# One level of Strassen in the MLP's up-projection: 19 of 22 tile pairs per layer

## The chip, the core and the metric

One core of a Trainium2 chip runs the whole trunk as one program. The metric is the device time in microseconds. TensorE multiplies matrices, VectorE and ScalarE do the elementwise work, GpSimd is nearly unused, and SyncE issues the transfers.

## The reference, cut to what matters

Two encoder layers over 512 tokens of width 1024 in float32. Each layer has four token mixers, one output projection, and then a gated MLP:

```python
h = rms_norm(x, ffn_norm_g[i])
u = depthwise_conv(h @ w_up, conv_w, conv_b)     # 1024 -> 2 x 2816, width-3 conv over tokens
gate, up = jnp.split(u, 2, axis=-1)
x = x + (silu(gate) * up) @ w_down               # 2816 -> 1024
```

A final RMSNorm closes the trunk.

## The kernel before, in words

Everything lies transposed: channels in the 128 partitions, the 512 tokens in the free dimension. A float32 product is made of three reduced-precision products (`float32r`): each operand is split into a high half (`hi`, a cast) and a low half (`lo`, the difference, always on VectorE), and hi x hi, hi x lo and lo x hi are accumulated in PSUM (`mm3`). The cast (`copy`) may go to ScalarE or VectorE, as the planner likes.

The MLP of a layer (`ffn`) goes through 22 pairs of up tiles: tile 2j is the gate's 128 channels, tile 2j+1 the matching up channels. `up_tile` loads 512 KB of weights (128 x 1024), splits them, does 8 x 3 products of 128x512 on the not yet normalised input, scales the result out of PSUM by the norm factor `r` (`evac_r`), and applies the width-3 convolution (one ScalarE and two VectorE instructions). `pair` applies silu, multiplies, and splits the product for the down projection. After every part of `PARTS = (5, 6, 6, 5)` pairs, `down` multiplies that part with its rows of the down weights, 8 output tiles, and adds each into the residual `x`. The last part of the last layer is done by `finish`, in two halves of 256 tokens, with the final norm. During layer 0's MLP a generator (`side`, `s5_prep`) records the preparation of layer 1's state-space weights after the pairs.

The order of issue is not the recorded order. Class `_Plan` records all instructions and then makes a list schedule: each instruction has a cost from `_cost`, ten forward and backward passes set priorities, and a buffer can be taken only if one is free. Buffers are 49 small slots of SBUF (`NSLOT`, up to 515 words a partition), 19 large ones (`NBIG`, 1024 words and a little more), tiny ones and 8 PSUM banks; weights have caps on how many are alive (`CAPS`). Each engine then runs its part in that order. All instructions are emitted from one line, L527, so groups of the profile are told apart by tiles (`v_s` a small slot, `v_b` a large one, `v_t` a tiny one, `bank` PSUM, `xs__65` the residual, `vec__67` per-channel vectors) and by shape.

Of the kernel before, what the change touches and what calls it, by code (L numbers as in the profile page):

```python
# [17 lines left out]
P = 128  # L18
D = 1024
S = 512  # L20
# [3 lines left out]
NPAIR = DFF // P  # L24
PARTS = (5, 6, 6, 5)
OUTP = ((3,), (0, 1, 2))
CAPS = (3, 5, 5)
ORDER = ("SGCMpsgcym", "SGCMsgcym")
EARLY = (4, 5)
# [25 lines left out]
CSTW = _off  # L55
NSLOT = 49
NBIG = 19
SLOTW = S + 3
# [8 lines left out]
class _Ap:  # L67
# [19 lines left out]
    def window(self, dims, offset):  # L87
        """A view with its own strides."""
        return _Ap(self.base, self.chain + (("window", (dims, offset), {}),), _window(self.proto, dims, offset))
# [31 lines left out]
class _Plan:  # L121
    """Records instructions, then issues them in the order of a list schedule.

    Buffers live in arenas of SBUF and in the banks of PSUM from their first write to their last use;
    Tile derives every wait from the order of issue."""

# [73 lines left out]
    def tiled(self, mms):  # L200
        """Matrix products in column tiles of the array, which run side by side."""
        d = max(_cost("T", *m)[4] for m in mms) + 53.0 * (len(mms) - 1)
        return self.add([("T", "group", mms, {}, d, 0.0, 0.0)])
# [38 lines left out]
    def settle(self):  # L242
        """Classes of the buffers where the instructions run in the order of recording."""
        left, users, home = dict(self.limit), {}, {}
# [62 lines left out]
    def forward(self, prio, ref, home, horizon):  # L307
        """One list schedule. ref is an order that fits the buffers: an instruction may run ahead of it
        only where the rest of ref still fits, so that no schedule gets stuck."""
        import bisect  # L310
# [49 lines left out]
        def fits(op):  # L360
            """The classes for the buffers that op would take, or None."""
            got, need, upto = [], {}, {}
# [185 lines left out]
def _cost(e, fn, a, k):  # L548
    n = _free(a[0])
    dma = 0.0  # L550
    if e == "T":
        if fn == "transpose":
            d = 109.0
        elif a[1].proto.dtype == F32R:
            d = max(n, 256) / 2.4 + 3.0
        else:
            d = 4.0 * max(n, 128) / 2.4 + 4.0
# [33 lines left out]
def trunk_kernel(  # L591
# [31 lines left out]
    fing_ = const.tile([P, KT], F32, name="fing_")  # L623
    vec_ = const.tile([P, L, VECW], F32, name="vec_")
    slots = ctx.enter_context(tc.tile_pool(name="slots", bufs=1))
    banks = [psp.tile([P, S], F32, name=f"bank{i}") for i in range(8)]
# [14 lines left out]
    def ps(shape=(P, S)):  # L641
        return plan.buf("ps", shape, F32)
# [14 lines left out]
    for k in range(KT):  # L657
        lead.append(X.dma_start(x[k], xT[k * P:(k + 1) * P, :]))
    fing = plan.fixed(fing_[:, :])
    X.dma_start(fing, fin_g)  # L660

# [10 lines left out]
    def wget(src, n, cap=True):  # L672
        raw = sb(F32, (P, n), ("raw", CAPS[0]) if cap else None)
        hi = sb(F32R, (P, n), ("whi", CAPS[1]) if cap else None)
        lo = sb(F32R, (P, n), ("wlo", CAPS[2]) if cap else None)
        plan.loaded = X.dma_start(raw, src)
        copy(hi, raw)
        V.tensor_sub(lo, raw, hi.bitcast(F32))
        return hi, lo
# [40 lines left out]
    def colsum(acc, mat=None):  # L720
        """Sums over the partitions, in every partition."""
        p_ = ps(acc.shape)
        T.matmul(p_, ones if mat is None else mat, acc)
        return p_
# [377 lines left out]
    def attend(scores, vt):  # L1102
        """Two heads; their outputs side by side in the partitions."""
        pt = [[b4(F32, (P, 2, S)) for _ in range(2)] for _ in range(2)]
# [35 lines left out]
    def group_norm(l, grp, y):  # L1140
        """y is the group, but twice that for group 0."""
        r = rstd(sumsq(y), 1024 if grp == 0 else 256)
# [14 lines left out]
    def mixing(l):  # L1157
# [224 lines left out]
        for grps in OUTP:  # L1382
# [3 lines left out]
            for m in range(KT):  # L1386
# [3 lines left out]
                V.tensor_add(x[m], x[m], p_)  # L1390

    def ffn(l, side):
        xh, xl, r = prenorm(l, "ffn_g")
        fw, _ = VEC["fc_w"]
        fb, _ = VEC["fc_b"]

        def up_tile(i):
            w = wget(w_up[l, i], KT * P)
            p_ = ps()
            mm3(p_, w, range(KT), xh, xl, P, P)  # L1400
            u = evac_r(p_, r)

            def cw(k):
                return vecs[l][:, fw + 3 * i + k:fw + 3 * i + k + 1]

# [6 lines left out]
        def pair(j):  # L1412
            g_ = up_tile(2 * j)
            u_ = up_tile(2 * j + 1)
            A.activation(g_, g_, AF.Silu)
            V.tensor_mul(g_, g_, u_)
            return split(g_)
# [13 lines left out]
        def finish(k0, n):  # L1431
            """The last part of the last layer and the norm after it, in two halves of the tokens."""
            ph = {k: prods[k0 + k][0] for k in range(n)}
# [25 lines left out]
        for n in PARTS:  # L1459
            for j in range(n):  # L1460
                prods.append(pair(base + j))
                next(side, None)
                if j == 1 and pend is not None:
                    down(*pend)
                    pend = None
# [160 lines left out]
```

## Time and profile before

| | |
|---|---|
| device time, median of 3 runs | 1248.66 us (1248.66 to 1249.28) |
| span of the profiled execution | 1248.9 us |
| TensorE / VectorE / ScalarE busy | 98% / 74% / 49% of the span |
| HBM read, over the span | 118.96 MB, 106 GB/s with writes |

The profiled execution has its span alone as its time; it lies 0.2 us above the median of the runs. Busy time of TensorE is that of pipelined instructions, so what a product costs is read from many of them in a row, not from the duration of one.

### The profile page before, as it was taken

Reading aid. Unit: us, or ns where it says so; the run is one execution under the profiler, and the core shown is the slowest. Engines: PE = TensorE matmul, PEld = TensorE weight load, DVE = VectorE, ACT = ScalarE, POOL = GpSimd, SP = SyncE. Lnnn points to the kernel's source line nnn. Section 1 sums busy time; section 2 is a strip of 40 time slices with the busy share of each in tenths; the row PEclk is TensorE's granted clock in tenths of the full one; section 3 lists DMA queues with packets and bytes.
Section 4 is the critical chain, followed back from the end, with each engine's and each line's share of the span. In section 5 each row is a group of like instructions: output and inputs, shape, how many; then the busy total and the mean of one; then the engine's idle time right before and its main releaser. Section 6 shows DMA issues by size and latency. Waiting matters only on the chain.

```text
span 1248.9 us, 15868 instructions
## 1 busy us (share of the span) xinstructions
PE 1222.4 (98%) x5824; PEld 937.8 (75%) x5824; DVE 926.8 (74%) x1706; ACT 615.2 (49%) x983; POOL 6.9 (1%) x27
## 2 busy tenths in 40 slices
PE   7999899999999999999999999999999999999996
PEld 5875456878888878888888756668888888888886
DVE  8889988868899665665677998887666656557465
ACT  6448689654443352333352666985533333234223
POOL 0000000000000000000000000000000000000000
PEclk9999999999999999999999999999999999999999
DMA  8559461332223332432555156234223332322211
GB/s 303 148 187 268 107 156 36 134 119 89 71 77 101 101 131 92 123 95 73 187 188 179 53 140 148 64 102 133 87 67 99 109 96 89 99 102 76 83 45 68
DMA packets 71662, 144.38 MB, mean 116 GB/s; under 512 B 20256, under 2 KB 28960, under 8 KB 71456
## 3 DMA queue, kind: packets, MB, share of 16 engines
q1 hardware_dynamic: 71584, 143.37, 37.5%
q8 instruction: 46, 0.75, 0.2%
q14 instruction: 32, 0.26, 0.1%
HBM read 118.96 MB, written 13.89 MB: 106 GB/s over the span
## 4 chain that ended last, share of the span: by engine, by line
PE 88%; DVE 5%; ACT 3%; DMA 1%; issue 1%; SPq 1%; ACTq 0%; DVEq 0%
PE bank L527 88%; DVE v_s L527 4%; ACT v_s L527 2%; DVE v_b L527 1%; DMA v_b<-v_b 1%; ACT L527 1%; SPq L527 1%; ACT v_b L527 1%; DVE v_t L527 0%; DMA xs__65<-in_xT_dram 0%; DMA v_s<-y_d 0%; ACTq L1621 0%; DVEq L1621 0%; ACTq L527 0%
## 5 line engine op out<-in xcount | busy, mean ns | idle before, releaser
L527 PE MATMUL bank<-v_s,v_b 128*128 128x512 f32 (+3 forms) x4594 | 1041.0, 396 | 11.6 <-ACT v_b L527 8.6
L527 PEld LDWEIGHTS bank<-v_s,v_b 128*128 128x128 f32 (+2 forms) x4594 | 794.8, 183 | 219.4 <-issue 25.7
L527 DVE TENSOR_TENSOR v_b<-v_b,v_b 128x1024 fp32r<-128x1024 f32 (+4 forms) x208 | 217.2, 1051 | 33.2 <-PE bank L527 18.2
L527 ACT CAST v_b<-v_b 128x1024 fp32r<-128x1024 f32 (+2 forms) x184 | 168.8, 934 | 114.8 <-PE bank L527 85.1
L527 DVE TENSOR_TENSOR v_s<-v_s,v_s 128x512 f32<-128x512 f32 (+6 forms) x294 | 179.9, 627 | 26.1 <-ACT v_s L527 23.2
L527 DVE TENSOR_TENSOR v_s<-bank,v_s 128x512 f32<-128x512 f32 (+1 forms) x119 | 83.0, 701 | 139.6 <-PE bank L527 137.5
L527 ACT ACTIVATE v_s<-v_s,vec__67 128x512 f32<-128x512 f32 x87 | 71.0, 817 | 195.3 <-DVE v_s L527 192.2
L527 DVE SCALAR_TENSOR_TENSOR v_s<-v_s,vec__67,v_s 128x511 f32<-128x511 f32 (+8 forms) x201 | 148.6, 746 | 15.3 <-ACT v_s L527 9.7
L527 ACT ACTIVATE v_s<-v_s 128x512 f32<-128x512 f32 (+2 forms) x124 | 71.1, 587 | 80.3 <-DVE v_s L527 79.4
L527 DVE TENSOR_TENSOR xs__65<-xs__65,bank 128x512 f32<-128x512 f32 x88 | 59.5, 682 | 61.5 <-PE bank L527 61.5
L527 ACT CAST v_s<-v_s 128x512 fp32r<-128x512 f32 (+1 forms) x70 | 40.0, 585 | 72.9 <-DVE v_s L527 71.4
L527 ACT ACT_TABLE_LOAD x52 | 66.7, 1283 | 15.7 <-DVE v_s L527 7.6
L527 PE MATMUL bank<-v_b,v_b 96*128 96x512 f32 (+5 forms) x264 | 74.1, 450 | 0.0
L527 PE MATMUL bank<-c_sb,v_s 128*128 128x128 f32 x368 | 64.8, 278 | 1.3 <-ACT v_s L527 1.2
L527 PEld LDWEIGHTS bank<-c_sb,v_s 128*128 128x128 f32 x368 | 44.6, 140 | 27.5 <-issue 18.5
L527 PE MATMUL bank<-v_b,v_s 128*128 128x64 f32 (+4 forms) x268 | 60.7, 393 | 1.9 <-ACT v_s L527 1.2
L527 PE MATMUL bank<-v_s,v_s 128*64 128x128 f32 (+2 forms) x258 | 57.4, 348 | 1.4 <-ACT v_s L527 1.4
L527 ACT ACTIVATE v_s<-bank,v_t 128x512 f32<-128x512 f32 x68 | 46.5, 697 | 10.6 <-DVE v_t L527 10.5
L527 PEld LDWEIGHTS bank<-v_b,v_s 128*128 128x128 f32 (+1 forms) x268 | 34.0, 173 | 16.0 <-issue 7.7
L527 DVE TENSOR_REDUCE v_t<-bank 128x1 f32<-128x512 f32 x64 | 42.3, 681 | 4.4 <-PE bank L527 3.7
L527 PEld LDWEIGHTS bank<-v_b,v_b 96*128 96x128 f32 (+3 forms) x264 | 33.2, 165 | 16.5 <-issue 8.1
L527 PEld LDWEIGHTS bank<-v_s,v_s 128*128 128x128 f32 (+1 forms) x258 | 32.1, 165 | 14.9 <-issue 5.7
(82 smaller groups left out, 517.9 us busy)
## 6 DMA issues: line engine op xcount, KB each, us to landing
v_b<-in_w_up_dram SPq DMA_DIRECT2D x88, 512.0 KB
v_b<-in_w_in_dram SPq DMA_DIRECT2D x28, 512.0 KB
v_b<-in_w_dn_dram SPq DMA_DIRECT2D x32, 384.0 KB
v_b<-in_w_dn_dram SPq DMA_DIRECT2D x32, 320.0 KB
v_b<-v_b SPq DMA_DIRECT2D x24, 256.0 KB
v_b<-in_w_out_dram SPq DMA_DIRECT2D x16, 384.0 KB
v_s<-x_d SPq DMA_DIRECT2D x22, 257.5 KB
v_s<-wt_d SPq DMA_DIRECT2D x15, 256.0 KB
```

The source lines that it names most:

```text
L527: self.issued(op, getattr(eng[e], fn)(*[res(z) for z in a], **{n: res(z) for n, z in k.items()}))
```

## The change

Of the 22 pairs of a layer the first three (`DIRECT`) stay as they are, with their weights loaded and split in blocks of 128 x 512. For each of the other 19, the pair's weights are a 2 x 2 matrix of blocks (two tiles by two halves of the 1024 inputs) and the input is a 2 x 2 matrix (two halves of the inputs by two halves of the tokens, 256 each). Seven block products replace eight (Winograd's form of Strassen): four sums of weight blocks are made per pair, and the sums of the input blocks (`operands`) once per layer, on the normalised input. Each product is 4 x 3 products of 128x256. The results are put together in PSUM, by ScalarE copies and by VectorE additions. The up tile comes out negative, and its convolution weights are negated once per layer (`nfw`). The down projection runs in 6 parts, (4, 4, 4, 4, 3, 3). There are 51 small and 22 large slots, new caps for the blocks' weights, and the planner's cost of a product is 0.4453 ns per column + 4 ns instead of 1/2.4 + 3. The scratch memory for descriptors is set to 2048.

```diff
-PARTS = (5, 6, 6, 5)
+PARTS = (4, 4, 4, 4, 3, 3)
+DIRECT = 3
+WCAPS = (10, 9, 9)
-NSLOT = 49
-NBIG = 19
+NSLOT = 51
+NBIG = 22
...
-            d = max(n, 256) / 2.4 + 3.0
+            d = 0.4453 * max(n, 256) + 4.0
...
+    def blocks(l, j):
+        w = [[sb(F32, (P, 512), ("sw", WCAPS[0])) for _ in range(2)] for _ in range(2)]
+        for i in range(2):
+            for h in range(2):
+                X.dma_start(w[i][h], w_up[l, 2 * j + i, :, 512 * h:512 * h + 512])
+        return w
...
+        V.tensor_scalar(nfw, vecs[l][:, fw:fw + 6 * NPAIR], -1.0, None, ALU.mult)
+        H = S // 2
+        CW = ("sh", WCAPS[1]), ("sl", WCAPS[2])
+        def operands():
+            q = {}
+            for kh, nh in ((0, 0), (0, 1), (1, 0), (1, 1)):
+                t_ = q[kh, nh] = b4(shape=(P, 4, H))
+                for k in range(4):
+                    V.scalar_tensor_tensor(t_[:, k], x[4 * kh + k][:, H * nh:H * nh + H], vcol(l, "ffn_g", 4 * kh + k),
+                                           r[:, H * nh:H * nh + H], ALU.mult, ALU.mult)
+            b11, b12, b21, b22 = q[0, 0], q[0, 1], q[1, 0], q[1, 1]
+            n1, n2, t4 = (b4(shape=(P, 4, H)) for _ in range(3))
+            V.tensor_sub(n1, b11, b12)
+            f11 = halves(b11)
+            V.scalar_tensor_tensor(n2, n1, -1.0, b22, ALU.mult, ALU.subtract)
+            fn1 = halves(n1)
+            V.scalar_tensor_tensor(t4, n2, -1.0, b21, ALU.mult, ALU.subtract)
+            f21, fn2 = halves(b21), halves(n2)
+            V.tensor_sub(b12, b22, b12)
+            return dict(b11=f11, b21=f21, n1=fn1, n2=fn2, b22=halves(b22), t3=halves(b12), t4=halves(t4))
+        def product(out, w, f, start):
+            for k in range(4):
+                sl = slice(k * P, k * P + P)
+                T.matmul(out, w[0][:, sl], f[0][:, k], start=start and k == 0, stop=False, skip_group_check=True)
+                T.matmul(out, w[0][:, sl], f[1][:, k], start=False, stop=False, skip_group_check=True)
+                T.matmul(out, w[1][:, sl], f[0][:, k], start=False, stop=(k == 3), skip_group_check=True)
+        def quarters(j):
+            a, c = blocks(l, j)
+            s1, s2_, s3, s4 = (sb(F32, (P, 512), ("sw", WCAPS[0])) for _ in range(4))
+            V.tensor_add(s1, c[0], c[1])
+            V.tensor_add(s2_, s1, a[0])
+            V.tensor_add(s3, a[0], c[0])
+            V.tensor_add(s4, s2_, a[1])
+            w11, w12, w1, w2, w4, w3, w22 = (halves(z, *CW) for z in (a[0], a[1], s1, s2_, s4, s3, c[1]))
+            g_, u_ = s2(), s2()
+            xb, yb, zb = (ps((P, H)) for _ in range(3))
+            product(xb, w11, ops["b11"], True)
+            A.activation(g_[:, 0:H], xb, AF.Copy)
+            product(zb, w12, ops["b21"], True)
+            V.tensor_add(g_[:, 0:H], g_[:, 0:H], zb)
+            product(yb, w1, ops["n1"], True)
+            A.activation(u_[:, H:S], yb, AF.Copy)
+            product(xb, w2, ops["n2"], False)
+            A.activation(g_[:, H:S], xb, AF.Copy)
+            product(yb, w4, ops["b22"], False)
+            V.tensor_add(g_[:, H:S], g_[:, H:S], yb)
+            product(xb, w3, ops["t3"], False)
+            V.tensor_add(u_[:, H:S], u_[:, H:S], xb)
+            product(xb, w22, ops["t4"], False)
+            A.activation(u_[:, 0:H], xb, AF.Copy)
+            return g_, u_
...
         def pair(j):
-            g_ = up_tile(2 * j)
-            u_ = up_tile(2 * j + 1)
+            g_, u_ = straight(j) if j < DIRECT else quarters(j)
+            g_ = spread(2 * j, g_, False)
+            u_ = spread(2 * j + 1, u_, j >= DIRECT)
...
             for j in range(n):
+                if base + j == 1:
+                    ops = operands()
                 prods.append(pair(base + j))
...
-    nc = _bacc.Bacc("TRN2", target_bir_lowering=False, num_devices=1)
+    nc = _bacc.Bacc("TRN2", target_bir_lowering=False, num_devices=1, dynamic_dma_scratch_size=2048)
```

`halves(raw)` is the second half of the former `wget`: a cast to the high half and a VectorE difference to the low one. `straight` is the former pair of `up_tile` on blocks, `spread` the former convolution, with `nfw` in place of the weights where the tile is negative.

## Rows read from the trace of the kernel before

**Rows 1.** The page's head and its busy times.

```profile
span 1248.9 us, 15868 instructions
PE 1222.4 (98%) x5824; PEld 937.8 (75%) x5824; DVE 926.8 (74%) x1706; ACT 615.2 (49%) x983; POOL 6.9 (1%) x27
```

**Rows 2.** The chain of work that ended last: its shares by engine, and its two longest pieces (start us, length us, what).

```profile
PE 88%; DVE 5%; ACT 3%; DMA 1%; issue 1%; SPq 1%; ACTq 0%; DVEq 0%
...
194.93 492.06 PE bank L527 x2210
...
788.16 445.94 PE bank L527 x2051
```

**Rows 3.** Busy time of the engines in stretches: stretch, its length, PE, PEld, DVE, ACT, POOL in us (with instructions), granted clock, DMA share, GB/s.

```profile
280.00:360.00 80.00, 80.00 (x347) 64.72 (x346) 70.44 (x184) 37.92 (x56) 0.72 (x3) 1.00 0.27 84
...
240.00:685.00 445.00, 445.00 (x1987) 358.47 (x1985) 321.29 (x537) 179.52 (x262) 2.83 (x7) 1.00 0.37 117
640.00:685.00 45.00, 45.00 (x217) 36.57 (x215) 32.98 (x43) 16.46 (x22) 0.00 (x0) 1.00 0.63 206
685.00:720.00 35.00, 33.19 (x161) 25.68 (x158) 34.16 (x112) 21.79 (x37) 0.24 (x2) 1.00 0.17 48
685.00:845.00 160.00, 156.34 (x837) 105.54 (x834) 145.65 (x312) 118.47 (x217) 0.48 (x4) 1.00 0.38 100
845.00:1238.00 393.00, 392.74 (x1810) 322.85 (x1808) 242.87 (x337) 148.72 (x200) 0.00 (x0) 1.00 0.27 87
```

**Rows 4.** The products and weight loads of 900 to 1160 us, grouped: count, busy us, mean ns of one, idle us before them.

```profile
L527 PE MATMUL bank<-v_s,v_b 128*128 128x512 f32 x1122 | 260.5, 394 | 0.0
L527 PEld LDWEIGHTS bank<-v_s,v_b 128*128 128x128 f32 x1121 | 210.5, 188 | 49.7
```

**Rows 5.** In `finish`: a stretch with its busy times (columns as in rows 3); a run in the order of time (start us, length us, engine, instruction, count in a row); and, grouped over the span, all products of that shape (count, busy us, mean ns of one, idle us before them).

```profile
1216.00:1229.00 13.00, 13.00 (x112) 13.00 (x111) 6.57 (x17) 3.92 (x10) 0.00 (x0) 1.00 0.00 1
...
1229.91 7.62 PEld L527 LDWEIGHTS bank<-v_s,v_b 128*128 128x128 f32 x63
1229.94 7.79 PE L527 MATMUL bank<-v_s,v_b 128*128 128x256 f32 x63
...
L527 PE MATMUL bank<-v_s,v_b 128*128 128x256 f32 x240 | 30.4, 282 | 0.0
```

**Rows 6.** The order of time on VectorE in a stretch without idle time, and one run of eight: start us, length us.

```profile
850.82 0.95 DVE L527 TENSOR_TENSOR v_b<-v_b,v_b 128x768 fp32r<-128x768 f32 x1
851.69 0.68 DVE L527 TENSOR_TENSOR v_s<-v_s,v_s 128x512 f32<-128x512 f32 x1
852.30 0.69 DVE L527 TENSOR_TENSOR xs__65<-xs__65,bank 128x512 f32<-128x512 f32 x1
852.90 0.75 DVE L527 SCALAR_TENSOR_TENSOR v_s<-xs__65,vec__67,v_s 128x512 fp32r<-128x512 f32 x1
853.57 1.22 DVE L527 TENSOR_TENSOR v_b<-v_b,v_b 128x1024 fp32r<-128x1024 f32 x1
854.70 0.69 DVE L527 TENSOR_TENSOR v_s<-v_s,v_s 128x512 f32<-128x512 f32 x1
...
1241.99 3.25 DVE L527 SCALAR_TENSOR_TENSOR v_s<-v_s,fing__66,v_s 128x256 f32<-128x256 f32 x8 [2.27 <-ACT v_s L527]
```

**Rows 7.** Groups of VectorE instructions over the span, shapes kept apart: count, busy us, mean ns of one, idle us before them.

```profile
L527 DVE TENSOR_TENSOR v_b<-v_b,v_b 128x640 fp32r<-128x640 f32 x32 | 26.0, 819 | 8.4 <-issue 4.1 <-PE bank L527 3.9 <-ACT v_b L527 0.2
L527 DVE SCALAR_TENSOR_TENSOR v_s<-v_s,fing__66,v_s 128x256 f32<-128x256 f32 x16 | 6.7, 476 | 2.3 <-ACT v_s L527 2.3
L527 DVE TENSOR_TENSOR v_s<-xs__65,bank 128x256 f32<-128x256 f32 x16 | 6.4, 418 | 8.3 <-PE bank L527 8.3
L527 DVE SCALAR_TENSOR_TENSOR v_s<-v_s,v_s 128x512 f32<-128x512 f32 x4 | 4.6, 1155 | 0.0
```

**Rows 8.** The same for ScalarE.

```profile
L527 ACT CAST v_b<-v_b 128x1024 fp32r<-128x1024 f32 x108 | 111.4, 1041 | 80.6 <-PE bank L527 60.4 <-DVE v_b L527 13.7 <-issue 5.8
L527 ACT CAST v_s<-v_s 128x512 fp32r<-128x512 f32 x59 | 36.3, 620 | 71.7 <-DVE v_s L527 71.4
L527 ACT COPY v_s<-bank 128x224 f32<-128x224 f32 x7 | 2.4, 347 | 7.2 <-PE bank L527 3.1 <-DVE v_s L527 2.6 <-issue 1.5
```

**Rows 9.** The transfer queue of the page (packets, MB, share of 16 engines' span), and SyncE's issues of up weights (duration ns least/median/most, first and last start).

```profile
q1 hardware_dynamic: 71584, 143.37, 37.5%
...
L527 SPq DMA_DIRECT2D v_b<-in_w_up_dram x88: 327/328/490, 218.4 to 1172.2; - x88
```

**Rows 10.** The order of time at the start of layer 1's MLP: the last additions into x, the norm factor on ScalarE (its last step, from 875.94), the first scaling of an up tile.

```profile
869.18 0.68 DVE L527 TENSOR_TENSOR xs__65<-xs__65,bank 128x512 f32<-128x512 f32 x1
873.33 17.05 PE L527 MATMUL bank<-v_s,v_b 128*128 128x512 f32 x71
875.94 0.63 ACT L527 ACTIVATE v_s<-v_s 128x512 f32<-128x512 f32 x1
878.87 0.69 DVE L527 TENSOR_TENSOR v_s<-bank,v_s 128x512 f32<-128x512 f32 x1 [5.95 <-PE bank L527]
```

**Rows 11.** What VectorE waited for in 240 to 685 us: us in total, times, longest.

```profile
DVE v_s L527 <- PE bank L527: 56.6, 23, 7.6
DVE xs__65 L527 <- PE bank L527: 34.6, 14, 7.5
DVE v_s L527 <- ACT v_s L527: 11.8, 14, 1.6
DVE v_b L527 <- issue: 7.7, 2, 4.1
DVE v_b L527 <- PE bank L527: 6.9, 6, 3.5
DVE v_b L527 <- ACT v_b L527: 0.6, 3, 0.3
DVE v_s L527 <- ACT v_b L527: 0.5, 1, 0.5
```

More of the change, by code (lines that the diff above doesn't have):

```diff
@@ L624, in trunk_kernel @@
     vec_ = const.tile([P, L, VECW], F32, name="vec_")
+    nfw_ = const.tile([P, 6 * NPAIR], F32, name="nfw_")
     slots = ctx.enter_context(tc.tile_pool(name="slots", bufs=1))
@@ L659, in trunk_kernel @@
     fing = plan.fixed(fing_[:, :])
+    nfw = plan.fixed(nfw_[:, :])
     X.dma_start(fing, fin_g)
@@ L673, in wget, with halves @@
         raw = sb(F32, (P, n), ("raw", CAPS[0]) if cap else None)
-        hi = sb(F32R, (P, n), ("whi", CAPS[1]) if cap else None)
-        lo = sb(F32R, (P, n), ("wlo", CAPS[2]) if cap else None)
         plan.loaded = X.dma_start(raw, src)
+        return halves(raw, ("whi", CAPS[1]) if cap else None, ("wlo", CAPS[2]) if cap else None)
+    def halves(raw, ch=None, cl=None):
+        hi, lo = sb(F32R, raw.shape, ch), sb(F32R, raw.shape, cl)
         copy(hi, raw)
@@ L1395, in ffn @@
         fb, _ = VEC["fc_b"]
[L1397 to L1401, printed above, removed]
+        V.tensor_scalar(nfw, vecs[l][:, fw:fw + 6 * NPAIR], -1.0, None, ALU.mult)
[18 more added lines that the diff above has]
+            return dict(b11=f11, b21=f21, n1=fn1, n2=fn2, b22=halves(b22), t3=halves(b12), t4=halves(t4))
@@ new lines, in straight @@
+        def straight(j):
+            out = []
+            for w in blocks(l, j):
+                w = [halves(z, *CW) for z in w]
+                p_ = ps()
+                for k in range(KT):
+                    sl = slice(k % 4 * P, k % 4 * P + P)
+                    wh, wl = w[k // 4]
+                    T.matmul(p_, wh[:, sl], xh[k], start=(k == 0), stop=False)
+                    T.matmul(p_, wh[:, sl], xl[k], start=False, stop=False)
+                    T.matmul(p_, wl[:, sl], xh[k], start=False, stop=(k == KT - 1))
+                out.append(evac_r(p_, r))
+            return out
@@ L1403, in cw, with spread @@
+        def spread(i, u, neg):
             def cw(k):
-                return vecs[l][:, fw + 3 * i + k:fw + 3 * i + k + 1]
+                z = 3 * i + k
+                return nfw[:, z:z + 1] if neg else vecs[l][:, fw + z:fw + z + 1]
             y = s2()
```

## The prediction, made before the change was run

> **What bounds the kernel now.** I read the page's busy shares first. TensorE is busy 98% of the 1248.9 us span, VectorE 74%, ScalarE 49% [rows 1]. Then the chain of work that ended last: 88% of it is TensorE, and two unbroken TensorE pieces, from 195 to 687 us and from 788 to 1234 us, make up 938 us [rows 2]. They cover both MLPs (240 to about 640 and 845 to 1238 us) and the layer-1 projections. So in the MLPs a TensorE microsecond saved is a microsecond of span, as long as nothing else becomes the bound. What else could be is read from the stretch table [rows 3]: in the layer-1 MLP VectorE is busy 242.9 of 393 us and ScalarE 148.7; in 240 to 685 us, the layer-0 MLP plus the first projections of layer 1, VectorE is busy 321.3 of 445. The difference is the preparation of layer 1's state-space weights, which is recorded as side work of the layer-0 MLP. Between 685 and 845 us VectorE already has 145.7 of 160, so that stretch can take little more.
>
> **TensorE's price.** In 900 to 1160 us there is nothing but 128x512 products: 1122 in 260.55 us, 0.232 us each [rows 4]. Products of 256 columns stand in the trace only at the end of the kernel, in `finish`: from 1216 to 1229 us nothing but them, 112 in 13.0 us, 0.116 each with the weight loads busy throughout; a later run of 63 takes 7.79 us, 0.124 each; all 240 are busy for 30.4 us, 0.127 with their interruptions [rows 5]. I take 0.118, just above the unbroken stretch, since the new products have this very pattern (two with the high half, one with the low) and run by the thousand without a pause. A pair of up tiles costs 48 x 0.232 = 11.15 us before and 7 x 4 x 3 = 84 products of 256 columns after, 84 x 0.118 = 9.91 us: 1.24 us less, 23.5 per layer for 19 pairs, 47 in all. At 0.116 the pair saves 1.4 us (53 in all), at 0.127 0.5 us (18 in all). The granted clock is 1.00, the 2.4 GHz level, in every one of these stretches [rows 3, 5].
> The Trainium skill (TensorE: Matmul & The Clock Gate, "What overlaps and what doesn't" with "LDWEIGHTS") speaks against the change: a weight load takes columns / 1.2, 107 ns for 128, and is hidden under a running product only where the row groups differ, which they never do here. By that rule, with 512 columns in 213 ns by the same page, 48 x (213 + 107) = 15.4 us would become 84 x (107 + 107) = 18.0 us and the kernel would lose some 99 us. The trace does not bear it out: 210.5 us of weight loads lie under 260.5 us in which the products never pause [rows 4]. It is rival E.
> The last part of layer 1 has 3 pairs instead of 5: 96 products of 256 columns become 48 of 512, 11.6 against 11.1 us, 0.5 us less.
>
> **VectorE's price.** A VectorE instruction's recorded time overlaps the next one's by about 0.08 us, so I price by start to start: 512 elements of a sum 0.60 to 0.61, scalar-tensor-tensor 0.67, 1024 elements 1.13 us [rows 6]; 256 elements 0.42 - 0.08 = 0.34, scalar-tensor-tensor of 256 (3.25 - 0.48)/7 = 0.40, 640 and 768 elements 0.74 and 0.87 [rows 6, 7]. Per Strassen pair VectorE gains 4 weight sums (2.40), 7 low halves of 512 instead of 2 of 1024 (4.20 - 2.26), and 3 sums of 256 out of PSUM instead of 2 scalings of 512 (1.01 - 1.20): 4.15 us, 78.8 per layer. Direct pairs: 4 halves for 2, 0.4. Down in 6 parts: 16 more additions into x (9.6) and low halves 32 x 0.60 + 16 x 0.47 against 16 x 0.74 + 16 x 0.87 (1.0): 10.6. Operands of the products: 16 scaled quarters of 256 (6.4), two differences and two scalar-tensor-tensors of 1024 (4.6, the latter bounded below by the plain sum's 1.13 and above by 2 x 1.16 of the slowest 512 row [rows 7]; I take the plain sum, the layout is plain too) and 7 low halves of 1024 (7.9): 18.9. Sum: 108.7 us per layer.
> The Trainium skill (VectorE: DVE Perf Modes, "The TRN2 errata") puts an instruction at (N + 151)/0.96 ns, 0.16 us of fixed cost each. The recorded 0.69 us agrees, the start-to-start 0.60 does not; with the 256 further instructions per layer (10 x 19 Strassen, 6 direct, 32 down, 28 operands) the page's fixed cost would add 22 us more per layer. It is rival F.
>
> **ScalarE and DMA** I cost at nothing. ScalarE gets 7 casts of 512 (4.35) and 4 copies of 256 out of PSUM (about 0.37 each, from the 224-wide row) for 2 casts of 1024 (2.08) [rows 8]: 3.75 x 19 + 7.3 for the operands = 79 us, to 60% of the layer-1 MLP. Up weights come as 4 transfers of 256 KB per pair for 2 of 512, down weights as 96 for 64: 108 more issues of 0.33 us on SyncE over the whole run, which does nothing else, with the same bytes and the queue's packets at 37.5% [rows 9]. If weights came late, VectorE's sums would be late, then the products.
>
> **Putting the two together, layer 1.** TensorE needs 393 - 23.5 - 0.5 = 369 us; VectorE 242.9 + 108.7 = 351.6, 95% of it. TensorE stays the bound, except at the start: the products need the norm factor r, which lands at 876.6 us, and then the 18.9 us of operands [rows 10]. Before r TensorE has the last output tiles, which end at about 868 us, and then 33 us of direct tiles (to 901). From 876 to 901 VectorE must do operands, 6 scalings (3.6) and the first weight sums and halves (6.6): 29 us in 25. I charge 4 us (0 to 10). Gain 20.
> **Layer 0.** In 240 to 685 us TensorE needs 445 - 23.5 = 421.5; VectorE 321.3 + 108.7 = 430. Some of the 321 is the 0.08 us tail that idle gaps leave uncovered: 63 waits, 5.0 us [rows 11]. So 425, and VectorE is the bound here, by little. The best share VectorE shows is 34.2 of 35 us, 97.6% [rows 3]; at 97% it needs 438.6 us. Gain 6.4 of the 23.5. What is late then: the sums, so weight halves, so the products, and TensorE idles with waits on VectorE.
> Total: 1248.9 - 20 - 6.4 = 1222.5 on the profiled execution's span; the median of the runs, 1248.66, lies 0.2 below that span. I say 1222.
>
> **Rivals.**
> A. TensorE stays the bound throughout: the planner spreads the state-space preparation into 640 to 685 us and the scalar engine takes VectorE's remaining copies. For it: 12 us of VectorE are free in 640 to 685, and VectorE reached 97.6%. Against: 425 in 421.5 leaves no slack, and the projections' own work follows there. Even at 100% VectorE limits layer 0 to a gain of 20; with 24 in layer 1 that is 1205.
> B. Start of each MLP: operands come in one block and TensorE waits 10 us in layer 1 instead of the 4 I charge, and 8 in layer 0 where VectorE's lateness hides part: 1222 + 14 = 1236. For it: r is one instant, everything waits for it; against: three direct pairs are there to run meanwhile.
> C. Slower: VectorE does not hold 97%. SBUF slots are the place: 14 of 22 large slots hold operands through the whole MLP, weights of a pair want 8 + 7 + 7 of 10 + 9 + 9 capped slots, so VectorE can run hardly a quarter of a pair ahead, and layer 0 also keeps the state-space buffers. At the 91% that VectorE holds in 685 to 845 us, layer 0 needs 430/0.91 = 472.5 (27.5 more than before) and layer 1 386 (7 less): 1269. It decides from the share at which layer 0 gives back layer 1's 20 us: 430/465 = 92.5%. For it: long stretches stand at 88 to 91% [rows 3]. Against: those shares were reached where TensorE was the bound, not VectorE.
> D. The same, with the share within a point of that 92.5%: no change.
> E. Slower: weight loads, not columns, set the pace. A load is recorded at 0.188 us beside 512-column products [rows 4]; were that its length beside short products, a pair would cost 84 x 0.188 = 15.8 us, 4.6 more, and the kernel 1249 + 38 x 4.6 = 1425. Against: 63 loads in a row took 7.62 us, 0.121 each [rows 5].
> F. Slower: each further VectorE instruction costs its 0.08 us tail too: 256 x 0.08 = 20.5 us per layer, so 450/0.97 = 464 in layer 0 (19 more than before) and 372/0.97 = 384 in layer 1 (9 less): 1259. Against: the starts in rows 6.
>
> **How the numbers follow.** Forecast 0.51, its own range 1211 to 1235 (layer 1 gains 14 to 24, layer 0 nothing to 14). A 0.18, B 0.09, D 0.05, C 0.14, E 0.01, F 0.02. 0.2% of this kernel is 2.5 us, about what a measurement can tell from no change. Faster is forecast + A + B = 0.78, same 0.05, slower 0.17 (C, E, F). The range for 8 in 10 reaches to A's 1205 and, with the price of a product at 0.127 or VectorE at 92%, up to 1252.
>
> **What would show it.** Right: 256-column products at 0.116 to 0.12 us start to start in unbroken runs; VectorE over 95% in the layer-0 MLP and about 95% in layer 1; TensorE's idle time mostly in the layer-0 MLP, released by VectorE; layer 1's MLP some 20 us shorter, layer 0's about 6. Wrong: a product price at 0.127 or over (the gain more than halves), TensorE idle in both MLPs with VectorE under 92% (C), no idle in either (A), or one gap of 10 us behind each r (B).

## The result and the profile after

The kernel after takes 1238.18 us (median, 1237.13 to 1239.29) beside 1248.97 us of the kernel before on the same chip: ratio 0.9906, interval 0.9892 to 0.9921. It is faster by 10.8 us where some 26 were forecast (20 + 6.4); the direction was right, the size was not. The page of after, beside [rows 1, 2]:

```profile
span 1235.3 us, 19839 instructions
...
PE 1194.5 (97%) x7144; PEld 976.1 (79%) x7144; DVE 1126.1 (91%) x2220; ACT 751.4 (61%) x1383; POOL 6.9 (1%) x27
...
PE 75%; DVE 17%; ACT 3%; issue 2%; DMA 2%; SPq 0%; DVEq 0%; ACTq 0%
```

VectorE gained 199 us of work (926.8 to 1126.1) and now holds 17% of the chain of work that ended last instead of 5%. TensorE's products run as priced: this is one unbroken run of 80 new ones in the order of time (start, length, count in a row), (9.70 - 0.28)/79 = 0.119 us from start to start.

```profile
919.27 9.70 PE L529 MATMUL bank<-v_b,v_s 128*128 128x256 f32 x80
```

Where the time went is read by stage. A stage ends here where its last addition into x starts on VectorE. The five stretches of after, columns as in [rows 3]:

```profile
0.00:265.00 265.00, 253.04 (x1302) 171.40 (x1303) 235.91 (x547) 177.91 (x326) 3.57 (x16) 1.00 0.55 170
265.00:630.00 365.00, 359.70 (x2344) 323.19 (x2343) 357.10 (x700) 219.83 (x418) 2.83 (x7) 0.99 0.34 109
630.00:866.00 236.00, 230.89 (x1159) 160.41 (x1158) 201.65 (x399) 149.06 (x267) 0.49 (x4) 1.00 0.43 119
866.00:1205.00 339.00, 331.68 (x2194) 302.73 (x2192) 312.61 (x532) 191.11 (x348) 0.00 (x0) 0.99 0.28 87
1205.00:1235.30 30.30, 19.15 (x153) 18.35 (x151) 18.80 (x46) 13.50 (x25) 0.00 (x0) 0.86 0.21 70
```

This table gives the length of each stage in us for every kernel of this study, and its median time. Times of one kernel repeat within 0.9%, most within 0.5%, so a difference of 12 us or more between two kernels is theirs; the kernel before, run again beside the experiments, took 1250.3 to 1252.0 us there, and the ratios below are to these times. One of e5's four executions, at 1328.89 us with a granted clock of 0.844, was in a slower state and is left out of its median. The stages are those of the profiled execution, which in e1, e2 and e5 lay 4 to 7 us from the median (1269.4, 1267.7, 1257.6). Such an execution takes 1.8 to 2.4 us more than its span (1237.17 at 1235.3 for after).

| kernel | time | mixing 0 | MLP 0 | mixing 1 | MLP 1 | end |
|---|---|---|---|---|---|---|
| before | 1248.97 | 265.1 | 380.3 | 223.8 | 342.7 | 37.0 |
| after | 1238.18 | 265.2 | 365.1 | 235.4 | 339.8 | 29.9 |
| e1 before, new price | 1262.41 | 273.6 | 379.4 | 235.0 | 344.6 | 35.1 |
| e13 before, 0.418 | 1268.20 | 275.3 | 378.8 | 231.2 | 343.6 | 35.7 |
| e14 before, 0.414 | 1268.94 | 276.9 | 380.3 | 228.6 | 342.8 | 37.0 |
| e2 after, no Strassen | 1264.02 | 267.0 | 380.7 | 238.0 | 350.3 | 29.8 |
| e3 after, old price | 1253.77 | 269.5 | 348.4 | 259.4 | 341.8 | 29.9 |
| e9 after, 0.444 | 1243.96 | 261.8 | 371.5 | 236.5 | 338.6 | 30.3 |
| e5 after, 0.447 | 1262.80 | 264.5 | 385.3 | 235.2 | 340.5 | 30.1 |
| e6 after, mixing old price | 1254.75 | 275.9 | 375.9 | 230.3 | 340.7 | 30.2 |
| e4 after, no outer taps | 1231.83 | 265.2 | 365.8 | 235.5 | 333.1 | 29.9 |
| e8 after, one operand | 1215.03 | 267.6 | 343.8 | 240.8 | 328.9 | 29.9 |
| e10 after, no side work | 1242.15 | 275.9 | 363.9 | 231.7 | 340.1 | 29.9 |
| e7 after, sums on GpSimd | 1329.75 | 269.0 | 424.8 | 232.5 | 370.5 | 30.7 |
| e11 tuned a | 1218.68 | 263.4 | 354.8 | 238.2 | 331.8 | 29.8 |
| e12 tuned b | 1214.46 | 261.2 | 348.2 | 241.5 | 331.2 | 30.1 |
| e15 tuned b, no Strassen | 1261.82 | 260.6 | 380.6 | 237.4 | 350.4 | 30.5 |

After against before: layer 0's MLP gained 15.2 us, layer 1's mixing, whose instructions the change does not touch, lost 11.6 of it, and layer 1's MLP with the end gained 10.0 where 20 were forecast. The borders of the stages are not sharp, since the planner may issue work of one stage during another. Layer 1's mixing in before, columns as in [rows 3]:

```profile
645.00:869.00 224.00, 220.34 (x1132) 157.60 (x1131) 191.15 (x371) 144.19 (x251) 0.48 (x4) 1.00 0.42 119
```

In after it holds 27 more products and 28 more VectorE instructions (1159 and 399), so part of the 11.6 is work moved into it, at most 27 x 0.23 = 6 us of TensorE; layer 0's MLP and this mixing together went from 604.1 to 600.5 us. Two questions follow: what lengthened the mixing, and what took half of layer 1's gain.

### The profile page after: what moved, and what is told of

It reads as the page before. It is cut to its first block, busy times and chain, and to the rows that moved or that the text cites. A ratio compares the mean times of both kernels' runs of the same rounds, so it can differ in the third digit from the quotient of the medians.

```text
span 1235.3 us, 19839 instructions
## 1 busy us (share of the span) xinstructions
PE 1194.5 (97%) x7144; PEld 976.1 (79%) x7144; DVE 1126.1 (91%) x2220; ACT 751.4 (61%) x1383; POOL 6.9 (1%) x27
## 4 chain that ended last, share of the span: by engine, by line
PE 75%; DVE 17%; ACT 3%; issue 2%; DMA 2%; SPq 0%; DVEq 0%; ACTq 0%
PE bank L529 75%; DVE v_s L529 13%; DVE v_b L529 3%; ACT v_s L529 2%; ACT L529 1%; DVE xs__65 L529 1%; DMA y_d<-v_b 0%; DMA v_s<-y_d 0%; ACT v_b L529 0%; DMA xs__65<-in_xT_dram 0%; DMA v_b<-in_w_out_dram 0%; DMA v_b<-in_w_dn_dram 0%; DMA v_s<-in_w_dn_dram 0%; SPq L529 0%; DVE v_t L529 0%
## 5 line engine op out<-in xcount | busy, mean ns | idle before, releaser
L529 PE MATMUL bank<-v_b,v_s 128*128 128x256 f32 (+3 forms) x3390 | 582.0, 294 | 9.6 <-DVE xs__65 L529 8.7
L529 PEld LDWEIGHTS bank<-v_b,v_s 128*128 128x128 f32 (+1 forms) x3390 | 480.3, 189 | 37.4 <-DVE xs__65 L529 10.3
L529 DVE TENSOR_TENSOR v_s<-v_s,v_s 128x512 fp32r<-128x512 f32 (+6 forms) x709 | 440.8, 654 | 10.6 <-ACT v_s L529 6.7
L529 PE MATMUL bank<-v_s,v_s 128*128 128x512 f32 (+2 forms) x1455 | 433.1, 379 | 7.2 <-ACT v_s L529 2.6
L529 PE MATMUL bank<-v_s,v_b 128*128 128x512 f32 (+3 forms) x1480 | 358.2, 414 | 10.1 <-ACT v_b L529 8.9
L529 PEld LDWEIGHTS bank<-v_s,v_s 128*128 128x128 f32 (+1 forms) x1455 | 250.0, 185 | 62.5 <-issue 5.3
L529 PEld LDWEIGHTS bank<-v_s,v_b 128*128 128x128 f32 (+2 forms) x1480 | 221.5, 172 | 96.0 <-issue 36.3
L529 ACT CAST v_s<-v_s 128x512 fp32r<-128x512 f32 (+1 forms) x386 | 223.5, 604 | 104.4 <-DVE v_s L529 77.4
L529 PE MATMUL bank<-v_b,v_b 128*128 128x256 f32 (+6 forms) x379 | 107.2, 400 | 0.3 <-DVE xs__65 L529 0.3
L529 DVE TENSOR_TENSOR v_b<-v_b,v_b 128x1024 fp32r<-128x1024 f32 (+4 forms) x69 | 74.6, 1093 | 2.4 <-ACT v_b L529 2.4
L529 DVE TENSOR_TENSOR v_s<-v_s,bank 128x256 f32<-128x256 f32 x107 | 44.3, 418 | 13.7 <-PE bank L529 11.2
```

The lines of the kernel that those rows point to most:

```text
L529: self.issued(op, getattr(eng[e], fn)(*[res(z) for z in a], **{n: res(z) for n, z in k.items()}))
```

## Experiments: the planner's price and the order that comes of it

**The price alone, and everything but Strassen.** e1 is the kernel before with the new price; e2 is the kernel after with all 22 pairs direct and no operands.

```diff
-            d = max(n, 256) / 2.4 + 3.0
+            d = 0.4453 * max(n, 256) + 4.0
```


> The kernel before with one edit: the planner's cost of a product (0.4453 ns a column + 4 instead of 1/2.4 + 3). No work is added or removed, only the order of issue can move. Theory V (what is missing from the forecast was lost to VectorE: it is late at the start of layer 1's MLP and fills layer 0's): no change, 1246 to 1251 us, and the stretch between the last addition of layer 0's MLP and the last of layer 1's mixing stays near 223.8 us. Rival P (the planner: a new price makes another order, and the 11.6 us by which that stretch is longer after the change come from the order): 1255 us or more, and the stretch is some 10 us longer here too.

```diff
-DIRECT = 3
+DIRECT = 22
...
-                if base + j == 1:
-                    ops = operands()
```


> The changed kernel with all 22 pairs direct: blocks of weights, down in 6 parts, new slots, caps and price, but no Strassen product and no operands. Theory V: TensorE is the bound again, 1247 to 1252 us, so Strassen alone is worth some 11 us. Rival P: 1258 us or more, so that Strassen alone is worth 20 to 26 us as forecast and the rest of the change gives 10 to 15 back.

e1 is 12 us slower than before (ratio 1.0107, 1.0076 to 1.0138), e2 14 us (1.0113, 1.0092 to 1.0134). Both have the two MLPs of before, to 1 us together with the end, except that e2 has moved 7 us from the end into the last MLP with its shorter last part. What they lose is in the mixing stages: 8.5 + 11.2 us in e1, 1.9 + 14.2 in e2. Rival P's readings hold in both. So layer 1's mixing gets as long without any Strassen product, in e1 also without work moved into it (1134 products and 369 VectorE instructions in 235 us):

```profile
653.00:888.00 235.00, 231.23 (x1134) 158.70 (x1133) 190.69 (x369) 153.60 (x259) 0.50 (x4) 0.99 0.39 111
```

And Strassen with its operands is worth 1264.0 - 1238.2 = 25.8 us against the kernel that differs in it alone (and in the order planned for it).

**Is it the price's value, or any change of the order?** e3 takes the old price back in the kernel after; e5 and e9 move the new one by 0.4% and 0.3%; e6 keeps the old one in the mixing stages (the price is switched at the start of `ffn` and back behind it); e13 and e14 move the old price in the kernel before.

```diff
-            d = 0.4453 * max(n, 256) + 4.0
+            d = max(n, 256) / 2.4 + 3.0
```


> The changed kernel with the planner's old cost of a product. Same instructions, another order. Theory V: within 4 us of the changed kernel's 1238. Rival P: at least 6 us away from it, in either direction; if the new price is what costs, 1228 or less.

```diff
-            d = 0.4453 * max(n, 256) + 4.0
+            d = 0.447 * max(n, 256) + 4.0
```


> The kernel after, with the planner's price of a product raised by another 0.4% (0.447 in place of 0.4453 per column), nothing else; the same instructions in another order. If the price matters by its truth (a better price makes a better order), the time stays within 3 us of the kernel after, 1235 to 1241 us. If the order that comes of a price is a matter of luck, the stages move by 5 to 20 us with the products at the same 0.118 and 0.232 us: I guess 1250 us, with the loss in layer 0's MLP (365 us in the kernel after, 375 to 382 here).

(0.444 in its place:)


> The kernel after, with the planner's price of a product 0.3% lower (0.444 in place of 0.4453 per column), nothing else: the third point of the series 0.444, 0.4453, 0.447. If the time followed the price's truth there would be a smooth curve through 1238 us at 0.4453 and 1263 at 0.447, so about 1220 us here. If it is luck in the order, there is no curve: 1235 to 1260 us, with layer 0's MLP at 365 to 385 us and layer 1's MLP unchanged at 340 us.

```diff
+RATE = [(1.0 / 2.4, 3.0)]
...
+            d = RATE[0][0] * max(n, 256) + RATE[0][1]
...
+        RATE[0] = (0.4453, 4.0)
...
+        RATE[0] = (1.0 / 2.4, 3.0)
```


> The kernel after, with the old price for the products of the mixing stages and the new one for those of the MLP. If the new price itself is what lengthens layer 1's mixing, that stage goes from 235 back to 224 us and the whole to about 1227 us. If the mixing's length comes from whatever order the planner falls into, the stage may stay at 230 to 240 us, and the others move by some us either way: 1230 to 1255 us.

```diff
-            d = max(n, 256) / 2.4 + 3.0
+            d = 0.418 * max(n, 256) + 3.0
```


> The kernel before with the price of a product at 0.418 per column in place of 0.4167 (0.3% more), nothing else. If the order of the kernel before is one of many alike, the time stays within 3 us of 1249. If it is better than its neighbours (a tuned kernel keeps the best of many orders), the mixing stages get longer with the MLP stages unchanged (380 and 343 us): 1253 to 1265 us.

(0.414 in its place:)


> The kernel before with the price at 0.414 per column (0.6% less), nothing else. The same two readings: 1246 to 1252 us, or 1253 to 1265 us with the MLP stages unchanged. If the truth of the price counted, this one and the last should lie on either side of 1249.

It is the order, not the price's truth. With prices of 0.444, 0.4453 and 0.447, less than 1% apart, the kernel after takes 1244.0, 1238.2 and 1262.8 us: layer 0's MLP is 371.5, 365.1 and 385.3 long, with the same instructions. e6 lost 16 us (1.0034 of before) though its mixing of layer 1 did get 5 us shorter: its first mixing and MLP got 10.7 and 10.8 longer. e3, at 1.0033 of before and 16 us above after, has layer 0's MLP 17 us shorter than after and the mixing behind it 24 longer, so the old price is not the better one. And the kernel before is no typical one: its price moved up or down gives 1268.2 and 1268.9 us (ratios 1.0136 and 1.0137, both intervals within 1.0119 to 1.0153), 16 to 17 us more, with the MLPs as they were and both above the 1265 that was expected at most. e1's 1262.4 stands beside them. The two mixing stages of e13, columns as in [rows 3]:

```profile
0.00:275.00 275.00, 258.95 (x1301) 172.72 (x1302) 228.37 (x530) 183.52 (x325) 3.57 (x16) 0.96 0.53 158
...
654.00:885.00 231.00, 227.38 (x1142) 157.89 (x1141) 188.63 (x366) 156.71 (x264) 0.49 (x4) 1.00 0.44 119
```

In the first TensorE is idle for 16 us, 3 more than in before, and the granted clock is 0.96 instead of 1.00. In the second it is idle for 3.6 us only; there its own busy time is the longer one, and which instructions make it so was not followed further.

So the kernel before had a better order than each of the four neighbours tried, by 12 to 17 us (e1, e13 and e14 differ from it in the price alone, e2 in buffers, caps, blocks and parts as well). Whoever touches an input of the planner draws another order; of the inputs only the price was varied by itself.

**What a bad order looks like.** e5's TensorE waits in layer 0's MLP (us in total, times, longest), its order of time there, and the two stretches with their granted clock:

```profile
PE bank L529 <- DVE xs__65 L529: 14.5, 3, 8.2
```

```profile
530.42 5.29 PE L529 MATMUL bank<-v_s,v_s 128*128 128x512 f32 x21
543.93 1.22 PE L529 MATMUL bank<-v_s,v_s 128*128 128x512 f32 x2 [8.21 <-DVE xs__65 L529]
```

```profile
520.00:560.00 40.00, 30.18 (x175) 24.05 (x175) 33.44 (x58) 18.87 (x41) 1.05 (x2) 0.91 0.24 77
560.00:600.00 40.00, 33.30 (x215) 28.15 (x214) 32.88 (x59) 18.58 (x48) 1.05 (x2) 0.91 0.26 85
```

TensorE has written its down products into the PSUM banks and cannot go on until VectorE adds them into x, which stand in VectorE's queue behind more than 20 us of weight sums, halves and taps. In the same 80 us VectorE itself is idle for 13.7 us: the two engines wait for each other in turns. The granted clock of both stretches is 0.91 on average, so part of each ran at 1.2 GHz. The kernel after has the same kind of wait in layer 0's MLP, but a shorter one, 3.1 us, and nearly all of its idle time there (4.8 of 5.3 us) is in this stretch:

```profile
520.00:560.00 40.00, 35.24 (x209) 29.04 (x207) 38.63 (x68) 17.50 (x39) 1.05 (x2) 0.91 0.24 73
```

## Experiments: VectorE's load

**Less load in the same order.** e4 issues the kernel after in its own order, but leaves out the outer convolution taps of the Strassen pairs (`t1` and `t2`, two VectorE instructions per tile: 152 x 0.67 = 102 us in all). They are planned and then skipped.

```diff
...
+            t1.skip = t2.skip = i >= 2 * DIRECT
...
+                if op.skip:
+                    continue
```


> The changed kernel in exactly its own order of issue, but the two VectorE instructions of the convolution's outer taps are not issued in Strassen pairs: 4 x 38 instructions of 0.66 us, 100 us of VectorE, are left out (the output is not the reference's). Theory V: the waits of TensorE for VectorE in both MLPs (8.3 us in 500 to 560, 9.9 us in 960 to 1000) go away, 1218 to 1224 us. Rival P, or a lack of slots or PSUM banks that the order itself fixes: 1232 us or more, since the order is the same.

It takes 1231.83 us (0.9855 of before), at the edge of rival P's reading: 6.7 us less in layer 1's MLP and nothing in layer 0's, where VectorE's share fell from 98% to 85%:

```profile
265.00:631.00 366.00, 361.23 (x2345) 325.19 (x2344) 312.71 (x624) 218.54 (x419) 2.83 (x7) 0.99 0.34 109
```

Its order of time at the wait in layer 0, VectorE and then TensorE:

```profile
529.72 0.69 DVE L531 TENSOR_TENSOR v_s<-v_s,v_b 128x512 f32<-128x512 f32 x1 [1.67 <-PE bank L531]
...
530.65 3.59 DVE L531 TENSOR_TENSOR v_s<-v_s,v_s 128x512 f32<-128x512 f32 x5
...
541.40 0.68 DVE L531 TENSOR_TENSOR xs__65<-xs__65,bank 128x512 f32<-128x512 f32 x1
```

```profile
542.14 0.80 PE L531 MATMUL bank<-v_b,v_s 128*128 128x256 f32 x2 [3.14 <-DVE xs__65 L531]
```

VectorE first waits for TensorE, then works for 11.7 us, nearly all of it weight sums, and the addition that frees the bank comes last. The wait is 3.1 us, as in the kernel after: in this place the order set it, not the load.

**The operands.** e8 computes one operand in place of seven; all seven products read it.

```diff
-            for kh, nh in ((0, 0), (0, 1), (1, 0), (1, 1)):
+            for kh, nh in ((0, 0),):
...
+            f11 = halves(q[0, 0])
+            return dict.fromkeys(("b11", "b21", "n1", "n2", "b22", "t3", "t4"), f11)
```


> The kernel after, with six of the seven Strassen operands left out: all seven products read the first one, so the block of VectorE work at the start of each MLP falls from 18.8 us to about 3 us a layer; the order is planned anew. By the prediction's step (4 us charged at the start of layer 1, nothing in layer 0 beyond VectorE's total) the time falls by 4 us in layer 1's MLP and at most 5 in layer 0: 1229 to 1234 us. If the block is worth what layer 1's MLP lost against the forecast (10 us), that stage falls from 340 to 330 us, layer 0's by as much again, and the whole to 1215 to 1222 us.

It takes 1215.03 us (0.9712 of before), as the second reading had it. Its MLPs, columns as in [rows 3]:

```profile
267.50:611.50 344.00, 344.00 (x2267) 314.25 (x2266) 339.33 (x673) 201.56 (x381) 2.30 (x6) 1.00 0.32 101
...
852.00:1181.00 329.00, 328.97 (x2201) 301.46 (x2200) 301.02 (x515) 181.77 (x339) 0.00 (x0) 1.00 0.29 88
```

TensorE has no pause in either. Layer 1's MLP with the end is 10.9 us shorter than after, and 20.9 shorter than before: the forecast's 24, before its charge of 4, is nearly all there. So the operands cost 10.9 us there. The order of e8 is another one too, but layer 1's MLP hardly depends on it: it takes 338.6 to 341.8 us in the five orders of the same instructions (after, e3, e5, e6, e9). Where the operands show in the kernel after is not at their place. Their first and longest runs on VectorE, the stretches behind them, TensorE's longest wait in 940 to 1000 us, VectorE's order of time at it, and who holds the chain of work from 923 to 980 us:

```profile
871.80 4.45 DVE L529 SCALAR_TENSOR_TENSOR v_b<-xs__65,vec__67,v_s 128x256 f32<-128x256 f32 x11 [0.68 <-ACT v_s L529]
...
885.55 4.63 DVE L529 TENSOR_TENSOR v_b<-v_b,v_b 128x1024 fp32r<-128x1024 f32 x4
```

```profile
865.00:965.00 100.00, 99.75 (x624) 88.79 (x624) 98.81 (x163) 65.00 (x111) 0.00 (x0) 1.00 0.27 87
...
965.00:985.00 20.00, 12.93 (x64) 10.96 (x63) 20.00 (x34) 8.15 (x15) 0.00 (x0) 0.83 0.34 110
```

```profile
PE bank L529 <- DVE xs__65 L529: 5.6, 1, 5.6
```

```profile
977.85 0.68 DVE L529 TENSOR_TENSOR v_s<-v_s,v_b 128x512 fp32r<-128x512 f32 x1
978.46 0.68 DVE L529 TENSOR_TENSOR v_s<-v_s,v_s 128x512 fp32r<-128x512 f32 x1
979.06 2.47 DVE L529 TENSOR_TENSOR xs__65<-xs__65,bank 128x512 f32<-128x512 f32 x4
```

```profile
by line: DVE v_s L529 52.7%; PE bank L529 22.1%; issue 11.8%; DVE v_b L529 5.8%; DMA v_s<-in_w_dn_dram 4.1%; ACT v_s L529 1.8%; DVE xs__65 L529 1.2%; ACT v_b L529 1.1%; DVEq L529 0.1%; SPq L529 0.0%; ACTq L529 0.0%
```

TensorE is busy for 99.75 of the first 100 us: direct tiles and the first Strassen pairs cover the operands. But VectorE runs 98.8 of them and stays behind: from 923 us on the chain, which until then is TensorE's alone, goes mostly over VectorE, and some 90 us after the operands its additions into x come too late. TensorE is idle for 7 of 20 us, and the granted clock of these 20 us is 0.83. In e8 the chain of the first 120 us of this MLP is TensorE's alone. Not all of the wait is the load's: e4, with fewer VectorE instructions in the order of after, still has 3.0 us of it.

**Side work left out.** e10 does not issue the preparation of layer 1's state space in layer 0's MLP (`side_work` plans it and skips it).

```diff
...
-        ffn(l, s5_prep(l + 1, -1e6) if l + 1 < L else iter(()))
+        ffn(l, side_work(l + 1) if l + 1 < L else iter(()))
```


> The kernel after in its own order of issue, but the preparation of layer 1's state space, which layer 0's MLP carries as side work, is not issued (about 37 us of VectorE, 12 of ScalarE, 10 of TensorE; layer 1 reads layer 0's prepared tensors, so its output is another one). If VectorE's backlog sets the pace of layer 0's MLP (its share is 98% there), the waits for the additions into x around 520 to 560 us go and the stage falls from 365 to about 350 us, TensorE's own work: total 1222 us. If the order fixes the stage whatever VectorE's load, as it seemed when the outer taps were left out, it loses only TensorE's 10 us: 355 us, total 1228.

1242.15 us, 4 more than after and by neither reading. The premise did not hold: layer 1 reads layer 0's prepared tensors, which now live longer, and the order is another one (the first mixing is already 275.9 long). It tells nothing of the load by itself, but that 30 us less of VectorE (327.2 of 363.9 us busy, 90%) bought 1 us of layer 0's MLP in that order.

**The sums on GpSimd.** e7 takes the four weight sums of each pair (s1, s2_, s3, s4) from VectorE.

```diff
-            V.tensor_add(s1, c[0], c[1])
+            GP.tensor_add(s1, c[0], c[1])
...
```


> The kernel after, with the four sums of weights of a Strassen pair on GpSimd, so that VectorE is rid of 76 of 418 instructions of 512 columns a layer, about 45 us a layer. If VectorE's backlog is what costs the first 120 us of layer 1's MLP, that stage loses its wait of 6 us and its low clock: 340 to 331 us, and the whole comes to 1224 to 1232 us. If VectorE is no bound there, the whole stays at 1235 to 1241. If GpSimd's reads and writes slow VectorE's, or its sums come late (about 1 us each if it takes twice VectorE's time), products wait for them: 1245 us or more.

1329.75 us (1.0626 of before), by the last of the three readings. Groups over the span (count, busy us, mean ns of one, idle before): GpSimd's sums and two of VectorE's groups in e7, then the same two in after:

```profile
L529 POOL TENSOR_TENSOR v_s<-v_s,v_s 128x512 f32<-128x512 f32 x95 | 164.6, 1739 | 528.0 <-PE bank L529 361.6 <-DVE v_s L529 113.7 <-issue 36.3
...
L529 DVE TENSOR_TENSOR v_s<-v_s,v_s 128x512 fp32r<-128x512 f32 x321 | 263.2, 838 | 11.1 <-PE bank L529 4.8 <-ACT v_s L529 3.8 <-POOL v_s L529 0.9
...
L529 DVE TENSOR_TENSOR xs__65<-xs__65,bank 128x512 f32<-128x512 f32 x120 | 81.2, 681 | 24.6 <-PE bank L529 24.6
```

```profile
L529 DVE TENSOR_TENSOR v_s<-v_s,v_s 128x512 fp32r<-128x512 f32 x341 | 227.4, 688 | 5.6 <-ACT v_s L529 2.9 <-PE bank L529 1.3 <-issue 0.5
...
L529 DVE TENSOR_TENSOR xs__65<-xs__65,bank 128x512 f32<-128x512 f32 x120 | 81.0, 683 | 20.4 <-PE bank L529 20.2
```

A sum takes 1.74 us there instead of 0.69, and VectorE's instructions slow from 688 to 838 ns where both inputs lie in SBUF, while those with one input in PSUM stay at 681. The Trainium skill (SBUF — State Buffer, "Who interferes with whom") has it so: a VectorE instruction with two inputs in SBUF contends with a GpSimd instruction that reads SBUF. The trace agrees. How much of the 91 us comes from that was not separated: the sums themselves come later too, TensorE waits 47 us in all for VectorE's tiles in small slots against 6.6 in after, and the order is another one. The two rows, e7 and after (us in total, times, longest):

```profile
PE bank L529 <- DVE v_s L529: 47.0, 30, 5.3
```

```profile
PE bank L529 <- DVE v_s L529: 6.6, 7, 2.0
```

## Experiments: a version that beats both

Both findings point one way: give VectorE less to do behind the operands, and look for an order instead of taking the first. e11 and e12 have 4 or 3 direct pairs in layer 0 and 6 in layer 1, fewer weight tiles alive (7 and 8), a smaller bound on running ahead (`HOLD`) and other prices (e11 0.4489 in the MLP and 0.4421 elsewhere, e12 0.4479 throughout); e15 is e12 without Strassen. The diff is that of e12.

```diff
-DIRECT = 3
+DIRECT = ((0, 1, 2), (0, 1, 2, 3, 4, 5))
...
-WCAPS = (10, 9, 9)
+WCAPS = (8, 9, 9)
+RATE = [(0.4479, 4.0)]
...
-    HOLD = 60000.0
+    HOLD = 20000.0
...
-            d = 0.4453 * max(n, 256) + 4.0
+            d = RATE[0][0] * max(n, 256) + RATE[0][1]
...
-            g_, u_ = straight(j) if j < DIRECT else quarters(j)
+            g_, u_ = straight(j) if j in DIRECT[l] else quarters(j)
...
```


> A version meant to be faster: 18 Strassen pairs in layer 0 and 16 in layer 1 (4 and 6 direct pairs first, so that VectorE has 4 and 12 us less to do when the operands are made), 7 tiles for the weights in place of 10, a shorter look ahead (20000 in place of 60000), product prices of 0.4489 in the MLP and 0.4421 elsewhere, chosen among many for its planned order. If VectorE's backlog after the operands is what layer 1 lost, its MLP falls from 340 to about 333 us; layer 0's MLP to about 355; the whole to 1215 to 1228 us. If fewer Strassen pairs only cost TensorE (1.24 us each for four pairs), 1240 us or more.

> The same with 3 and 6 direct pairs, 8 tiles for the weights and one price of 0.4479: layer 1's MLP 333 us as before; layer 0's MLP 350 us, its mixing of layer 1 some 8 us longer in exchange; the whole 1215 to 1230 us. If the price decided, 0.4479 should be as bad as 0.447 was: 1255 to 1265 us.

> The faster of the two tuned versions (tuned b) with all pairs direct and no Strassen operands, every other setting the same, planned anew. By the prediction's price of a pair (1.24 us), 19 pairs in layer 0 and 16 in layer 1 are worth 43 us if TensorE is the bound throughout, less what the operands cost: 1214 + 43 = 1257 us, with the MLP of layer 0 at 378 and of layer 1 at 350 us. If Strassen's gain were smaller and the settings did the rest, 1230 to 1245 us.

e11 takes 1218.68 us (0.9744, 0.9717 to 0.9771), e12 1214.46 (0.9713, 0.9696 to 0.9731): 24 us faster than the kernel after, 37 than the one before. e15 takes 1261.82 (1.0081), 5 more than expected. The MLPs of e12 and the last MLP of e15:

```profile
261.00:609.00 348.00, 347.37 (x2273) 316.10 (x2272) 343.09 (x679) 206.25 (x381) 1.78 (x5) 1.00 0.32 100
...
851.00:1182.00 331.00, 331.00 (x2088) 297.89 (x2087) 303.62 (x513) 179.18 (x322) 0.00 (x0) 1.00 0.28 90
```

```profile
879.00:1229.00 350.00, 350.00 (x1510) 283.08 (x1510) 234.80 (x375) 117.34 (x186) 0.00 (x0) 1.00 0.27 84
```

With no pause on TensorE in either, layer 1's MLP compares product price with product price: 380.9 us with the end in e15, 361.3 in e12, 19.6 for 16 pairs, 1.23 each. Over the whole kernel 35 pairs brought 47.4 us where 35 x 1.24 = 43.4 were expected; the 4 us more are less than orders differ by. The settings alone are no gain, since e15 is slower than before; but e15's order was not searched for, so the 37 us against before, which is the fastest kernel without Strassen here, are the safer figure. Which of e12's settings carries how much was not tried one by one; that the price of 0.4479 alone does it is unlikely, since 0.447 was the worst of three in the kernel after.

## Why the prediction was off

**TensorE's price: right.** 0.118 us was forecast, 0.119 measured, and 1.23 us a pair where TensorE is the bound (e12 against e15). Rival E is out. The Trainium skill's rule on weight loads (TensorE: Matmul & The Clock Gate, "What overlaps and what doesn't") would, by an estimate from that page's figures (107 ns for a load and 107 for the columns), make a run of 80 take 17 us. The measurement decides: 9.70, so here the rule does not hold.

**VectorE's price: right, a little high.** Layer 1's MLP has 312.6 us of VectorE against 211.6 in before (below): 101 more where 108.7 were summed, and 199 over both layers where 217 were. Rival F is out with it, and so is C: VectorE's shares are 98% and 92%, and layer 0 did not lose.

```profile
869.00:1212.00 343.00, 343.00 (x1493) 277.91 (x1492) 211.57 (x280) 125.36 (x161) 0.00 (x0) 1.00 0.28 89
```

**Layer 1, the term that was mis-sized.** "I charge 4 us (0 to 10)" for the start measured 10.9 (e8). The working compared VectorE's load with TensorE's cover up to 901 us and stopped there. But by its own sum VectorE has a share of 95% to hold behind it, so what it owes at 901 it can pay back only slowly. How much it owed was not measured; that it was still behind is shown by the chain on VectorE from 923 us and by TensorE's wait at 974 us, and the pause took the clock with it. The sign "TensorE's idle time mostly in the layer-0 MLP" failed by the same: 7.3 us are in layer 1's, 5.3 in layer 0's. Rival B had the size (10 us) and nearly the time (1236), but looked for a gap behind r, and there is none.

**Layer 0, a right sum in the wrong place.** "Gain 6.4" came out as 3.6 for MLP and mixing together, but as 15.2 less 11.6, in part by work moved over the stages' borders. The share was well read (357.1 of 365 us is 98%, 97 was taken). But the share was not what set the length: e4 took VectorE down to 85% in the same order and gained nothing there, e5 lost 20 us at 94%, and e12, with the same 19 Strassen pairs in layer 0, holds 98.6% and needs 589.7 us for the two stages where after needs 600.5. What two totals leave out is the order in which each engine meets the other's work. That the 6.4 and the 3.6 lie so near each other is luck.

**The step that was missing: the planner's price.** The prediction gave this edit no term and put the mixing stages at no change without a reason. The price is an input of the order, and the kernel before stood on an order 12 to 17 us better than the neighbours tried (e1, e2, e13, e14). The change lost that order; against e2, which lost it too, Strassen brought 25.8 us, the size forecast. That agreement is partly luck, since orders of the kernel after differ by 25 us (e9, after, e5).

**The end.** The forecast was made on the span; in spans the gain is 1248.9 - 1235.3 = 13.6, in medians 10.8, since the profiled execution of before stands for one that was 2 us slower than its median (span and 1.8 to 2.4 us more). Of the 12.8 us that are missing in spans, 10.0 are layer 1's MLP with the end and 2.8 layer 0's MLP with the mixing behind it.

**ScalarE and DMA at nothing: held.** ScalarE is busy 191 of 339 us in layer 1's MLP. In the two MLPs the chain has two transfers of down weights, 3.0 us at 442 and 2.4 us at 974, the second within TensorE's pause, but VectorE, which frees the bank, is busy throughout that pause. (The issues are 120 more, not 108: the direct pairs' weights come in blocks too.)

## What to carry to other kernels

In a kernel whose order comes from a list schedule, an edit of the planner's inputs redraws the whole order; changes of the price of under 1% moved the time here by 6 to 25 us. Make a neighbour of the old kernel the reference (the same edit without the idea), and charge the loss of a tuned order as a term of its own. Where two engines are both above 90%, do not only compare totals; follow what the second owes from the moment it falls behind to the wait that collects it, and add the clock that the pause costs. Then search orders and settings again before judging the idea: here that turned a gain of 11 us into 37.

## What the runs showed of the hardware

A pause of TensorE costs more than itself: behind waits of 5.6 us the granted clock of a 20 us stretch was 0.83, behind 8.2 us that of two stretches of 40 us 0.91 each (e5, with two shorter waits among them). Behind waits of 3 us it fell in one place and not in another: in e4 it was 0.74 in 540 to 560 us and 1.00 in 960 to 1000. GpSimd is no free second VectorE: with 152 sums of 512 columns on it, at 1.3 to 1.75 us each, the kernel took 91 us longer, and VectorE's low halves with both inputs in SBUF took 22% longer (838 ns against 688).
